# The decay gate's rank-16 stage: two-part weights side by side in one product, and the second factor in two float32r passes over 64 rows

## The chip, the cores and the metric

The kernel runs on one core of one Trainium2 chip. The metric is the time of one execution on the device in microseconds, the median over runs of the same kernel. TensorE's clock has two levels, 1.2 and 2.4 GHz; the profile gives the granted clock as a share of the upper one.

## The reference

A two-layer encoder trunk over 1024 positions and a model width of 1024, in float32. Layer 0 has two head groups (RWKV-7 time mixing and sparse attention). Layer 1 is gated linear attention (GLA) in chunks of 64 with 4 heads. Each layer ends in a residual sum and a layer norm. The change lies in the decay gate of layer 1:

```
p = h @ o_w_in
q_c, k_c, v_c, gd, g_c = split_cols(p, [512, 512, 1024, 16, 1024])
log_a = log_sigmoid(gd @ g2 + g_bias) / 16        # gd: 1024 x 16, g2: 16 x 512
b     = cumsum of log_a over the positions of a chunk
q_e, k_e = q * 128**-0.5 * exp(b), k * exp(-b)
```

So the gate is a product of rank 16: 1024 inputs to 16 numbers per position (the first factor), and these to 512 (the second factor), which then pass through a log-sigmoid, a running sum within each chunk, and two exponentials that scale the queries and keys.

## The kernel before, in words

Most large products are made in a two-part form: an operand is split into a high part rounded to float32r and the float32r remainder (`hh` and `hl` for the normed input of layer 1, `whi` and `wlo` for weights), and three products high*high, high*low and low*high are summed in PSUM. The helper `mm_fm` (lines 178 to 185) does this for a result with features on partitions: for each of 8 blocks of 128 inputs three matmuls, with the weights stationary and 512 positions streamed. `mm_tm` (lines 201 to 207) does it for a result with positions on partitions.

Layer 1 begins with the norm of layer 0 (row tile by row tile), then the first 512 columns of the values (`values(t, 0, ...)`), and then the part that the change touches, from line 1368 on:

- The 16 weight columns of the first factor are loaded to `w16` and split by a ScalarE cast (`h16`) and a VectorE subtraction (`l16`).
- `mm_fm` multiplies them with `hh` and `hl` for two halves of 512 positions: 2 x 8 x 3 = 48 matmuls with 16 columns of weights, into 16 partitions of a PSUM tile `dn`.
- ScalarE copies the 16 x 1024 result to `gdT` in plain float32 (line 1377), and `g2`, the second factor, is loaded to 16 partitions.
- For each of 4 heads two float32 matmuls over 16 rows (line 1387) give 128 x 1024 into another `dn` tile, of which there are three. ScalarE takes the absolute value (line 1390) and VectorE the minimum with zero (line 1391).
- The log-sigmoid follows on ScalarE as Exp (line 1393) and Ln (line 1395), on VectorE a subtraction, a scan, a copy and a second subtraction (lines 1397 to 1402), and on ScalarE two closing Exps (lines 1403 and 1404).
- The second 512 columns of the values, `values(t, 1, wv, "tr")`: 8 row tiles t0 to t7, each 24 matmuls into one of two PSUM banks `tr`, and a ScalarE copy out of the bank into `vg` (line 1331).
- The query and key products (lines 1414 to 1418), which VectorE multiplies by the exponentials on the way out of PSUM.

Weights come through `wload` (line 162): a DMA on SP's queue to `wraw` (three buffers), a ScalarE cast to `whi`, a GpSimd subtraction to `wlo` (twelve buffers each). The small loads `w16` and `g2` go through ScalarE's queue.

The program is written in this order, but a scheduler sets the order of instructions on each engine when the program is built: it takes them by readiness as its own model of time has it. Each engine then executes its list in order, so that a copy that stands behind other ScalarE work waits for it. The matmuls of the second factor come out between those of the values, and the copies of the values between the steps of the gate.

Of the kernel before, what the change touches and what calls it, by code (L numbers as in the profile page):

```python
# [8 lines left out]
F32 = mybir.dt.float32  # L9
F32R = mybir.dt.float32r  # L10
# [11 lines left out]
P = 128  # L22
SEQ = 1024
NT = 8
D = 1024
NK = 8
CH = 64
# [46 lines left out]
def trunk(ctx: ExitStack, tc: tile.TileContext, x, positions, e_w_in, a_mu, a_w0, a_w2, a_a0, a_a2,  # L74
          a_kk_scale, a_ka, a_rk, a_gn_g, a_gn_b, b_kv_norm_g, b_wuk, b_wuv, e_w_out, o_w_in, c_g2,
          c_g_bias, c_norm_g, o_w_out, ln_g, ln_b, out, dbg=None, stop=None):
    nc = tc.nc
    V, A, G, PE = nc.vector, nc.scalar, nc.gpsimd, nc.tensor
    f32 = lambda ap: ap.bitcast(F32)
# [56 lines left out]
    def dtile():  # L136
        return psum["pool"].tile([P, 1024], F32, name="dn", tag="dn", bufs=psum["dn"])

    def ptile(tag, bufs=None):
        return psum["pool"].tile([P, 512], F32, name=tag, tag=tag, bufs=psum["bank"].get(tag, 1))  # L140
# [37 lines left out]
    def mm_fm(pst, wb, cs, ah, al, half):  # L178

        sl = slice(half * 512, half * 512 + 512)  # L180
        for k in range(NK):
            wh, wl = wb[k]
            PE.matmul(pst, wh[:, cs], ah[:, k, sl], start=(k == 0), stop=False)  # L183
            PE.matmul(pst, wh[:, cs], al[:, k, sl], start=False, stop=False)  # L184
            PE.matmul(pst, wl[:, cs], ah[:, k, sl], start=False, stop=(k == NK - 1))  # L185
# [173 lines left out]
    for t in range(NT):  # L359
        pt = dtile()  # L360
# [12 lines left out]
    for t0 in (0, 4):  # L373
        pt = ptile("tr")
# [246 lines left out]
    def shifted(f, c0, j):  # L621
        o = st("sh", bufs=3)
        shift_out(o, proj(c0 + j * P), f + j)
        return o
# [4 lines left out]
    for j in range(3):  # L629
        for z in PG[2 * j]:  # L630
            gate(z)
        k, r, v = (shifted(f, c0, j) for f, c0 in ((4, C_K), (0, C_R), (8, C_V)))
# [89 lines left out]
    for i in range(2, NT):  # L722
# [3 lines left out]
        z = slice(i - 2, i - 1)  # L726
# [17 lines left out]
    k = shifted(4, C_K, j)  # L744
# [529 lines left out]
    for u in range(NT):  # L1274
        w = u + 2
# [39 lines left out]
    hh = hp.tile([P, NK, SEQ], F32R, name="hh")  # L1315
    hl = hp.tile([P, NK, SEQ], F32R, name="hl")
# [48 lines left out]
    lp = l_ctx.enter_context(tc.tile_pool(name="lp", bufs=1, side="right"))  # L1365


    w16 = lp.tile([P, NK, 16], F32, name="w16")
    nc.scalar.dma_start(w16, owi[:, O_GD:O_GD + 16].rearrange("(k p) c -> p k c", p=P))
    h16, l16 = lp.tile([P, NK, 16], F32R, name="h16"), lp.tile([P, NK, 16], F32R, name="l16")  # L1370
    A.copy(h16, w16)
    V.tensor_sub(l16, w16, f32(h16))
    pt = dtile()
    for half in range(2):
        mm_fm(pt[0:16, half * 512:half * 512 + 512], [(h16[:, k], l16[:, k]) for k in range(NK)], slice(0, 16), hh, hl, half)
    gdT = lp.tile([16, SEQ], F32, name="gdT")
    A.copy(gdT, pt[0:16, :])
    g2 = lp.tile([16, 512], F32, name="g2")
    nc.scalar.dma_start(g2, c_g2[0])
    m1 = lp.tile([P, SEQ], F32, name="m1")  # L1380
    V.memset(m1, 1.0)
    V.memset(m1.rearrange("p (c t) -> p c t", t=CH)[:, :, 0:1], 0.0)
# [1 line left out]
    for h in range(4):  # L1384
        pt = dtile()
        for half in range(2):
            PE.matmul(pt[:, half * 512:half * 512 + 512], g2[:, h * P:(h + 1) * P], gdT[:, half * 512:half * 512 + 512],
                      start=True, stop=True)
        bc = par[:, GBI + h:GBI + h + 1]
        A.activation(eb[:, h], pt, AF.Abs, bias=bc)  # L1390
        V.tensor_scalar(la[:, h], pt, bc, 0.0, op0=ALU.add, op1=ALU.min)
# [20 lines left out]
    for z, (c0, dst, ex) in enumerate(((O_Q, qg, la), (O_K, kg, eb))):  # L1412
        wb = wblock(w0p, owi, c0, 512, bufs=RB)
        for j in range(4):
            pt = dtile()
# [86 lines left out]
    for z in range(RB):  # L1502
        c, k = divmod(z, NK)
# [6 lines left out]
    for z in range(RB, 16):  # L1510
        c, k = divmod(z, NK)
# [57 lines left out]
```

## Time and profile before

| | |
|---|---|
| median of 3 runs | 1324.16 us (1319.51 to 1325.7) |
| profiled execution | 1315.61 us, its span 1313.9 us |
| TensorE busy | 1193.3 us, 91% of the span |
| VectorE busy | 789.9 us, 60% |
| ScalarE busy | 602.5 us, 46% |
| GpSimd busy | 442.2 us, 34% |
| mean granted clock of TensorE | 0.956 |

Instructions are named by engine (PE is TensorE's matmuls, PEld its weight loads, DVE is VectorE, ACT is ScalarE, POOL is GpSimd, SP the queue of DMAs), by the line of the kernel and by the tiles that they write and read, with digits left out of names: `h<-w` is `h16<-w16`, `tr<-whi,hh` a matmul of the values. A float32 product shows as two instructions. Matmuls are pipelined, so that their durations overlap: the time of one is read from the distance between two starts. In brackets stands the idle time of the engine before an instruction, and what ended it.

### The profile page before, as it was taken

The page shows a single profiled execution, that of the slowest core. Times are in us where ns is not written, and L with a number is a line of the kernel's source. Part 1 is how long each engine was busy: PE and PEld are TensorE (multiplying, and loading weights), DVE is VectorE, ACT ScalarE, POOL GpSimd, SP SyncE. Part 2 cuts the span into 40 slices and gives each one's busy share as a digit, 9 for nine tenths or more (in the row PEclk, how much of TensorE's full clock was granted, in tenths as well). Part 3 has the DMA queues.
Part 4 walks back from the last instruction along what each step waited for, and adds up shares of the span by engine and source line. Part 5 has one row for each costly group of instructions (what it writes and reads, how often), then busy time and mean ns, then how long its engine had stood idle before and what let it go on. Part 6 is the DMA issues. An engine that isn't in the chain of part 4 may idle for free.

```text
span 1313.9 us, 22069 instructions
## 1 busy us (share of the span) xinstructions
PE 1193.3 (91%) x8141; PEld 942.7 (72%) x8141; DVE 789.9 (60%) x1868; ACT 602.5 (46%) x1253; POOL 442.2 (34%) x749
## 2 busy tenths in 40 slices
PE   7998798899899977998988499999899999998997
PEld 6986586566666665777777388876588878887785
DVE  5246879999999546676776436680701025444666
ACT  5347777668742445666766421232920024333100
POOL 3324741453447433344455610333031231142000
PEclk9998899899899979998999599999999999999999
DMA  6102311432515487343542756652020120024221
GB/s 210 39 1 85 109 44 29 137 104 72 153 41 144 117 221 189 98 104 93 128 120 51 217 167 221 212 177 68 0 64 16 49 65 1 0 65 136 81 92 53
DMA packets 164780, 130.52 MB, mean 99 GB/s; under 512 B 61440, under 2 KB 138288, under 8 KB 164672
## 3 DMA queue, kind: packets, MB, share of 16 engines
q1 hardware_dynamic: 161872, 122.72, 32.5%
q10 hardware_dynamic: 2800, 6.39, 1.5%
q8 instruction: 64, 1.05, 0.3%
q14 instruction: 44, 0.36, 0.1%
HBM read 86.08 MB, written 42.99 MB: 98 GB/s over the span
## 4 chain that ended last, share of the span: by engine, by line
PE 47%; DVE 20%; issue 9%; DMA 8%; ACT 7%; POOL 6%; SPq 1%; DVEq 0%; POOLq 0%; ACTq 0%
DVE junk L686 7%; PE op L774 7%; PE s L774 7%; PE dn L183 3%; PE dn L185 3%; PE dn L184 3%; PE gt L207 2%; PE gt L205 2%; PE gt L206 2%; POOL wlo L92 2%; PE s L853 2%; DMA wraw<-in_e_w_in_dram 1%; PE po L876 1%; PE dn L1465 1%; DVE sc L420 1%
## 5 line engine op out<-in xcount | busy, mean ns | idle before, releaser
L92 POOL TENSOR_TENSOR wlo<-wraw,whi 128x256 fp32r<-128x256 f32 (+1 forms) x160 | 117.0, 762 | 259.8 <-ACT whi L168 217.0
L183 PE MATMUL dn<-xh,chi 128*128 128x512 f32 x336 | 137.0, 408 | 4.8 <-DVE sh L512 3.1
L185 PE MATMUL dn<-xh,clo 128*128 128x512 f32 x336 | 137.1, 408 | 0.0
L184 PE MATMUL dn<-xl,chi 128*128 128x512 f32 x336 | 135.8, 404 | 0.0
L168 ACT CAST whi<-wraw 128x512 fp32r<-128x512 f32 (+1 forms) x80 | 48.6, 612 | 139.3 <-PE dn L184 64.4
L183 PEld LDWEIGHTS dn<-xh,chi 128*128 128x128 f32 x336 | 65.6, 195 | 25.1 <-issue 6.4
L185 PEld LDWEIGHTS dn<-xh,clo 128*128 128x128 f32 x336 | 65.6, 195 | 20.3 <-issue 6.7
L92 POOL TENSOR_TENSOR clo<-craw,chi 128x256 fp32r<-128x256 f32 x84 | 77.5, 951 | 1.0
L184 PEld LDWEIGHTS dn<-xl,chi 128*128 128x128 f32 x336 | 65.3, 194 | 16.8 <-issue 3.5
L420 DVE SCALAR_TENSOR_TENSOR sc<-rl,wi_s,sc 128x384 f32<-128x384 f32 (+5 forms) x42 | 45.1, 1074 | 24.3 <-ACT rl L415 21.9
L826 DVE CUSTOM_DVE_ANT_0 p<-s,bias_s 128x512 f32<-128x512 f32 (+1 forms) x80 | 45.3, 593 | 20.9 <-PE s L825 20.5
L92 POOL TENSOR_TENSOR vg<-vg,sg 128x256 f32<-128x256 f32 x32 | 24.1, 775 | 99.7 <-DVE vg L1491 65.2
L834 ACT ACTIVATE p<-p,am 128x128 f32<-128x128 f32 (+7 forms) x64 | 49.6, 776 | 15.6 <-DVE am L832 11.1
L193 POOL CAST chi<-craw 128x1024 fp32r<-128x1024 f32 x21 | 22.7, 1080 | 97.0 <-PE dn L184 79.7
L686 DVE TENSOR_SCALAR_CACHE_REDUCE junk<-khi,Hc 128x384 bf16<-128x384 int16 (+1 forms) x64 | 51.9, 810 | 1.7
L686 DVE TENSOR_SCALAR_CACHE_REDUCE junk<-klo,Lc 128x384 bf16<-128x384 int16 (+1 forms) x64 | 51.8, 810 | 1.7
L853 PE MATMUL s<-ident,p 128*128 128x128 f32 x288 | 48.4, 293 | 4.1 <-ACT pT L855 3.2
L205 PE MATMUL gt<-whi,hh 128*128 128x512 f32 x128 | 51.9, 406 | 0.0
L774 PE MATMUL s<-whi,yh 128*128 128x512 f32 x128 | 51.2, 400 | 0.0
L774 PE MATMUL op<-whi,yh 128*128 128x512 f32 x128 | 51.2, 401 | 0.0
L207 PE MATMUL gt<-whi,hl 128*128 128x512 f32 x128 | 51.2, 400 | 0.0
L206 PE MATMUL gt<-wlo,hh 128*128 128x512 f32 x128 | 51.0, 399 | 0.0
(479 smaller groups left out, 3413.8 us busy)
## 6 DMA issues: line engine op xcount, KB each, us to landing
wraw<-in_o_w_in_dram SPq DMA_DIRECT2D x48, 256.0 KB
craw<-in_e_w_in_dram SPq DMA_DIRECT2D x21, 512.0 KB
xt<-in_x_dram SPq DMA_DIRECT2D x8, 512.0 KB
d_q<-qiT SPq DMA_DIRECT2D x8, 512.0 KB
d_ar<-ar SPq DMA_DIRECT2D x8, 512.0 KB
d_gate<-sg SPq DMA_DIRECT2D x8, 512.0 KB
qT<-d_q SPq DMA_DIRECT2D x8, 512.0 KB
AT<-d_ar SPq DMA_DIRECT2D x32, 128.0 KB
```

The costliest lines, as they stand in the source:

```text
L92: return [f(out[:, a:min(n, a + w)], *(z[:, a:min(n, a + w)] for z in ins)) for a in range(0, n, w)]
L183: PE.matmul(pst, wh[:, cs], ah[:, k, sl], start=(k == 0), stop=False)
L184: PE.matmul(pst, wh[:, cs], al[:, k, sl], start=False, stop=False)
L185: PE.matmul(pst, wl[:, cs], ah[:, k, sl], start=False, stop=(k == NK - 1))
L205: PE.matmul(pst, ah[:, k, sl], wh, start=(k == 0), stop=False)
L206: PE.matmul(pst, ah[:, k, sl], wl, start=False, stop=False)
L207: PE.matmul(pst, al[:, k, sl], wh, start=False, stop=(k == NK - 1))
L420: E.scalar_tensor_tensor(acc[:, a:b], r, w, acc[:, a:b], op0=ALU.mult, op1=ALU.add)
L686: V.tensor_scalar(junk[:, :n], x, c[:, z:z + 1], None, op0=ALU.is_ge, op1=ALU.add, accum_out=cnt[:, z:z + 1])
L774: ins = PE.matmul(pt, a[:, k, :], b, start=(k == 0 and z == 0), stop=(k == NK - 1 and z == 2))
L834: A.activation(ps[k][:, :n], ps[k][:, :n], AF.Exp, scale=0.125, bias=m[:, k:k + 1], accum_out=rsum[:, k:k + 1])
L853: inorder(PE.transpose(pt[:, j * P:(j + 1) * P], OUT[i]["ps"][2 * j + s][:, kt * P:(kt + 1) * P], ident))
```

## The change

The weights of the first factor stand in one tile `w64` of 64 columns: high part, low part, and both again. One product with `hh` and `hl` (32 matmuls) gives 64 rows: high times x, low times x, and these again, so that all four products of the parts are made. The 64 rows are then cut into a float32r operand `gdx`: rows 0 to 31 are the rounded values, rows 32 to 63 the remainder of the same values. The second factor is loaded four times, to 64 partitions, and split into `g2h` and `g2l`; each head sums two float32r passes over these 64 rows. The diff:

```
-    h16, l16 = lp.tile([P, NK, 16], F32R, name="h16"), lp.tile([P, NK, 16], F32R, name="l16")
-    A.copy(h16, w16)
-    V.tensor_sub(l16, w16, f32(h16))
+
+    w64 = lp.tile([P, NK, 4, 16], F32R, name="w64")
+    for z in (0, 2):
+        A.copy(w64[:, :, z], w16)
+        V.tensor_sub(w64[:, :, z + 1], w16, f32(w64[:, :, z]))
+
+    g2 = lp.tile([CH, 512], F32, name="g2")
+    nc.scalar.dma_start(g2, bass.AP(tensor=c_g2[0].tensor, offset=c_g2[0].offset, ap=[[0, 4], [512, 16], [1, 512]]))
+    g2h, g2l = lp.tile([CH, 512], F32R, name="g2h"), lp.tile([CH, 512], F32R, name="g2l")
+    A.copy(g2h, g2)
+    V.tensor_sub(g2l, g2, f32(g2h))
     pt = dtile()
     for half in range(2):
-        mm_fm(pt[0:16, half * 512:half * 512 + 512], [(h16[:, k], l16[:, k]) for k in range(NK)], slice(0, 16), hh, hl, half)
-    gdT = lp.tile([16, SEQ], F32, name="gdT")
-    A.copy(gdT, pt[0:16, :])
-    g2 = lp.tile([16, 512], F32, name="g2")
-    nc.scalar.dma_start(g2, c_g2[0])
+        sl = slice(half * 512, half * 512 + 512)
+        for k in range(NK):
+            for z, x_ in enumerate((hh, hl)):
+                PE.matmul(pt[0:CH, sl], w64[:, k].rearrange("p z c -> p (z c)"), x_[:, k, sl], start=(k == 0 and z == 0),
+                          stop=(k == NK - 1 and z == 1))
+
+    gdx = lp.tile([CH, SEQ], F32R, name="gdx")
+    gdh = lp.tile([CH, SEQ], F32R, name="gdh")
+    A.copy(gdh, pt[0:CH])
+    A.copy(gdx[0:32], pt[0:32])
+    V.tensor_sub(gdx[32:CH], pt[32:CH], f32(gdh[32:CH]))
...
         for half in range(2):
-            PE.matmul(pt[:, half * 512:half * 512 + 512], g2[:, h * P:(h + 1) * P], gdT[:, half * 512:half * 512 + 512],
-                      start=True, stop=True)
+            for z, w in enumerate((g2h, g2l)):
+                PE.matmul(pt[:, half * 512:half * 512 + 512], w[:, h * P:(h + 1) * P], gdx[:, half * 512:half * 512 + 512],
+                          start=(z == 0), stop=(z == 1))
```

## Rows read from the trace of the kernel before

**Rows 1.** The page's busy time, share of the span and instructions, TensorE first.

```profile
PE 1193.3 (91%) x8141; PEld 942.7 (72%) x8141; DVE 789.9 (60%) x1868; ACT 602.5 (46%) x1253; POOL 442.2 (34%) x749
```

**Rows 2.** Busy time by stretches; columns are named in the first line.

```profile
core 0: us, PE busy (x) PEld busy (x) DVE busy (x) ACT busy (x) POOL busy (x), PEclk, DMA share, GB/s
...
919.90:925.30 5.40, 5.40 (x14) 2.16 (x13) 1.39 (x2) 3.87 (x5) 0.00 (x0) 1.00 0.00 0
925.30:929.00 3.70, 3.70 (x10) 2.92 (x10) 2.58 (x3) 3.66 (x4) 0.00 (x0) 0.54 0.00 0
...
950.90:973.40 22.50, 22.46 (x96) 18.14 (x97) 1.36 (x4) 7.08 (x11) 5.14 (x7) 1.00 0.05 13
973.40:1062.00 88.60, 88.60 (x381) 71.04 (x379) 8.57 (x7) 10.42 (x17) 22.86 (x33) 1.00 0.18 48
1062.00:1196.00 134.00, 132.62 (x631) 111.43 (x630) 55.01 (x153) 44.45 (x126) 33.79 (x47) 1.00 0.10 30
```

**Rows 3.** TensorE's matmuls in order of time: start us, us, engine, line, tiles, shapes.

```profile
903.22 0.41 PE L183 MATMUL dn<-hh,h 128*16 128x512 f32 x1 [1.37 <-ACT vg L1331]
...
914.26 0.39 PE L205 MATMUL tr<-whi,hh 128*128 128x512 f32 x1
...
919.95 5.41 PE L1387 MATMUL dn<-gdT,g 16*128 16x512 f32 x12
...
926.05 0.63 PE L207 MATMUL tr<-whi,hl 128*128 128x512 f32 x1
...
930.98 1.98 PE L1387 MATMUL dn<-gdT,g 16*128 16x512 f32 x4
...
942.87 0.50 PE L205 MATMUL tr<-whi,hh 128*128 128x512 f32 x1 [1.78 <-ACT vg L1331]
...
950.94 0.50 PE L205 MATMUL tr<-whi,hh 128*128 128x512 f32 x1 [1.96 <-ACT vg L1331]
...
973.44 0.39 PE L184 MATMUL dn<-hl,whi 128*128 128x512 f32 x1
```

**Rows 4.** Matmuls by tile; ns min/median/max, first and last start.

```profile
L183 PE MATMUL dn<-hh,h x16: 388/388/410, 903.2 to 913.6; 128*16 128x512 f32 x16
...
L1387 PE MATMUL dn<-gdT,g x16: 587/587/692, 919.9 to 932.4; 16*128 16x512 f32 x16
```

**Rows 5.** ScalarE in order of time, columns as in rows 3.

```profile
896.28 0.59 ACT L1331 COPY vg<-ca 128x512 f32<-128x512 f32 x1 [5.01 <-PE ca L207]
...
914.51 1.00 ACT L1377 COPY gdT<-dn 16x1024 f32<-16x1024 f32 x1 [5.16 <-PE dn L185]
...
921.96 1.11 ACT L1390 ACTIVATE kg<-dn,par 128x1024 f32<-128x1024 f32 x1 [1.32 <-PE dn L1387]
...
925.18 1.28 ACT L1395 ACT_TABLE_LOAD   x1
926.48 1.06 ACT L1395 ACTIVATE kg<-kg 128x1024 f32<-128x1024 f32 x1
...
942.25 0.57 ACT L1331 COPY vg<-tr 128x512 f32<-128x512 f32 x1
...
950.32 0.56 ACT L1331 COPY vg<-tr 128x512 f32<-128x512 f32 x1
...
953.79 0.57 ACT L1331 COPY vg<-tr 128x512 f32<-128x512 f32 x1
```

**Rows 6.** ScalarE's groups by form: busy us, mean ns of one, idle before.

```profile
L1395 ACT ACT_TABLE_LOAD x4 | 5.1, 1283 | 0.1
...
L1393 ACT ACTIVATE kg<-kg 128x1024 f32<-128x1024 f32 x4 | 4.2, 1062 | 0.1
L1395 ACT ACTIVATE kg<-kg 128x1024 f32<-128x1024 f32 x4 | 4.2, 1059 | 0.0
...
L1393 ACT ACT_TABLE_LOAD x2 | 2.6, 1283 | 0.0
L1403 ACT ACT_TABLE_LOAD x2 | 2.6, 1283 | 0.0
```

**Rows 7.** VectorE in order of time, columns as in rows 3.

```profile
923.17 1.28 DVE L1391 TENSOR_SCALAR qg<-dn,par 128x1024 f32<-128x1024 f32 x1 [34.00 <-ACT kg L1390]
```

## The prediction

> **What bounds the kernel now.** First the busy shares: TensorE is busy for 1193.3 of 1313.9 us [rows 1], so the end moves with TensorE unless a wait elsewhere sets it. Then the table by stretches [rows 2]. The stage that the change touches lies between 903.22, where TensorE starts the first product, and 973.44, where the query product takes over. Behind it TensorE is busy for all 88.6 us from 973.4 to 1062 and for 132.6 of the next 134.0, and the weight loads there are released by TensorE's own matmuls, so I take what this stage gains or loses to reach the end in full. I call this stage S; its length is 70.22 us.
>
> The order of TensorE's work in S [rows 3]: 48 matmuls of the first product (903.22 to 914.26), the second half of the values (8 row tiles t0 to t7, 24 matmuls each), and inside these the second product, heads 0 to 2 at 919.95 and head 3 at 930.98. Twice TensorE stands idle inside S, before 942.87 (1.78 us) and before 950.94 (1.96 us), both times for ScalarE's copy of a values tile out of PSUM. There are two such banks, so t3 waits for the copy of t1 and t4 for that of t2.
>
> ScalarE is the second thing to read [rows 5, 6]. From 921.96 on it works without a break through the gate's chain: per head Abs, Exp, Ln and two closing Exps, 20 operations of some 1.05 us, and eight table loads of 1.28, because Exp and Ln come in turns. The copy of t1 stands behind 12 of these 20 and starts at 942.25, when TensorE has run through t2 and waits for it; that of t2 behind 17, at 950.32. So in S either TensorE's sum or ScalarE's chain can be what ends last, and the change shortens only the first directly.
>
> **The change part by part, against the profiled execution.** Its time is 1315.61 us with a span of 1313.9; the median of the three runs, 1324.16, is 8.55 higher, and my predicted time is that median less the gain.
>
> First product. Removed are 48 matmuls at (914.26 - 903.22) / 48 = 0.230 us each, 11.04 in all [rows 3, 4]. Added are 32, each with 64 columns of weights. Their streamed side, 512 columns, is unchanged, and matmuls with 16 columns (0.230) and with 128 columns (22.5 us for 96, so 0.234, [rows 2]) bound the new one from both sides. I take 0.230: 7.36 us, a gain of 3.68. At 0.234 it would be 0.13 less.
>
> Second product. Removed are 8 float32 products. Each shows as two instructions, 16 in all [rows 4], 12 of which run from 919.95 over 5.34 us and 4 from 930.98 over 1.91 (to the next values matmul); with the two steps of 0.1 us ahead of them 7.44 us. Added are 16 float32r matmuls with 64 rows of weights. No float32r matmul with 64 rows is in the trace. The 128-row ones at 0.234 are the nearest; the float32 instruction at 0.43 is the other bound (16 x 0.43 = 6.9). I take 0.233: 3.73 us, a gain of 3.71, with 0.5 as its lower bound.
>
> Clock. Behind heads 0 to 2 the granted clock falls to a mean of 0.54 from 925.3 to 929.0 [rows 2], which is the lower level of 1.2 GHz nearly throughout: nine values matmuls stand 0.427 us apart instead of 0.233 the second of them is in [rows 3]. What TensorE did before was float32 work on 16 of 128 rows for 5.4 us. The first product, which also fills only 16 of 128 columns, kept 2.4 GHz for 11 us. The change replaces the float32 stretch by 2.8 us of work on 64 rows. I take the fall to be gone: 9 x 0.194 = 1.75 us gained; nothing gained is the other bound, and a fall that stays is rival D.
>
> Operand preparation. Two casts and two subtractions in place of one each, a wider transfer of the second factor's weights, one cast and one subtraction of these. They fall between 886 and 897, where ScalarE sits idle for five us at a stretch ([rows 5], at 896.28) and VectorE for 34 [rows 7]; the product that needs them starts at 903.22. I cost them at nothing. Without that cover it would be some 1.5 us for ScalarE's three casts, at no more than the 0.58 us of a 512-column copy each.
>
> Between the products. One ScalarE copy of 1.00 us ([rows 5], at 914.51) becomes two copies of that size and a subtraction, which I put at 1.28 by the 1024-column VectorE operation out of PSUM [rows 7]. The rounding error part needs the first copy, so the operand is ready some 2.8 us behind the first product's end instead of 1.3. Queued behind the copies on ScalarE is nothing but the gate's chain. TensorE has t0 to do meanwhile, 24 x 0.233 = 5.6 us, as it had before, so this also costs nothing; if the second product were put directly behind the first, it would cost 2.8.
>
> Sum for TensorE alone: S becomes 7.36 + 3.73 + 192 x 0.2333 (44.8) = 55.9 us, and the values end at 959.1. Before, they ended at 973.44 less the four query matmuls (0.93) that had been pulled ahead, so 972.5. If no wait were left, the gain would be 13.4.
>
> What is late next: t1's copy. With the order of before, TensorE ends the first product at 910.6, t0 at 916.2, head 0 at 917.1, heads 0 to 2 at 919.0, t1 and head 3 at 925.5, t2 at 931.1. ScalarE's chain starts some 0.3 behind head 0 as now, at 917.4 instead of 921.96. What counts is how many chain operations stand ahead of t1's copy. Before, a head arrived every 1.72 us while Abs took 1.1, so each gap was filled by the next step of an older head, and this mixed Exp with Ln. With a head every 0.93 us the three Abs can follow one another, and then four Exps and four Lns group, with one table load instead of six ahead of t1's copy. In that order, 4 x 1.1 + 4 x 1.06 + 1.30 + 4 x 1.06 = 14.2 us and the copy's 0.5 [rows 5, 6] put its end at 932.1. TensorE then waits 1.0 us at t3, and t4 to t7 find their banks free. The values end at 932.1 + 5 x 5.6 = 960.1: a gain of 12.4. If the first head's closing Exps come ahead of the copy as they did before, that adds a load and two operations, 3.4 us, and the gain is 9.0. I take a value between them nearer to the first, 11.0: 1304.6 for a profiled execution, and 1313.2 against the median.
>
> The Trainium skill (ScalarE: Activation LUTs, section "What ACT_TABLE_LOAD costs") gives a switch of tables 1283 ns and a drain of some 1380 behind it. The trace has the 1.28 [rows 5], and the Ln behind it starts 1.30 us after the load does, so no drain shows here; by the page the one load ahead of the copy would cost 1.4 more and the upper gain would be 11.0 instead of 12.4.
>
> The Trainium skill (TensorE: Matmul & The Clock Gate, Part 3, "The mechanism") has weight loads overlap a running matmul only where their row groups differ. All loads here use the same rows as the matmul that runs, and yet matmuls stand 0.234 us apart with a load between each pair [rows 2], so the trace does not follow it; by the page the new 64-row matmuls would each wait for their load, by an estimate some 0.19 each from the load's share of that row (18.14 us for 97), 3.0 us in all, and the gain would be 8.0.
>
> **The rivals.**
>
> B, ScalarE's order stays as it is. Then the chain alone shifts, by 4.56 us: t1's copy ends at 938.3 (20.9 behind the start, as before), t2's at 946.3, t3's at 949.8. TensorE waits 7.2 us at t3 and 2.4 at t4, and the values end at 968.8: a gain of 3.7, 1320.4. For it: the order is made for the whole program and was close to alternating. Against it: that alternation came from the slow arrival of heads, which goes.
>
> C, slower: the copy of t1 falls behind the whole gate chain, which stands ahead of it in the program. Before, 12 of 20 operations were ahead of it, and 17 ahead of t2's. With all heads ready early nothing need leave a gap for it. 20 operations (21.3), eight loads (10.4) and the copy end at 917.4 + 32.2 = 949.6, t3 starts there, and the values end at 977.6: 5.1 longer, 1329.3. It decides once t1's copy ends later than 944.5, 27 us behind the chain's start. Against it: both early copies were placed soon after an operation of the chain had to wait for VectorE, and those waits stay.
>
> D, the clock still falls to 1.2 GHz around the second product: 16 x 0.194 = 3.1 there and 1.75 behind it are lost, the gain is 6.1, 1318.0. For it: this is the one place inside S where it falls. Against it: four times the rows and half the time.
>
> That the change doesn't do what it says (64-row float32r passes at the float32 price) is 3.2 off the gain, 1316.4, and lies inside the range.
>
> **How the numbers follow.** Forecast 0.56, with its own range of 9.0 to 13.4 gained, 1310.8 to 1315.2; B 0.20, C 0.12, D 0.12. 0.5% of the time is 6.6 us, about what a measurement of this kernel tells from no change. Faster by more: the forecast and a third of D, 0.60. Within it: B and the rest of D, 0.28. Slower: C, 0.12. The range runs from the full 13.4 with 3.8 for the spread of a median (the three runs lie 6.2 apart), 1307, to B with 2.6 of it, 1323, and leaves C out.
>
> **What would show it.** Right: 32 first-product matmuls in some 7.4 us; the second product's 16 at 0.233; no granted clock under 1.00 in S; two to four table loads in the chain instead of eight; at most one wait of TensorE for a values copy, under 4 us; the query product starting around 960 to 963. Wrong: a wait of 7 us at t3 with eight loads (B), a query product after 973 (C), values matmuls 0.43 apart (D), or a change outside S as large as the one inside.

## The result, and the profile after

The changed kernel takes 1308.98 us (median of 4 runs, 1301.1 to 1311.88) against 1323.2 us (4 runs, 1319.51 to 1325.7): a ratio of 0.9885, 95% interval 0.9836 to 0.9935. A second set on another occasion, 6 runs against 11, gave 1304.47 against 1317.18, a ratio of 0.9896 with 0.9875 to 0.9918. So the change saves some 14 us, 1.1%, with an interval from 0.8 to 1.25% by the narrower set.

The profiled execution of the changed kernel took 1311.88 us, only 3.7 less than that of before. The span and the engines' busy time, after:

```profile
span 1310.2 us, 22044 instructions
...
PE 1189.9 (91%) x8125; PEld 945.8 (72%) x8125; DVE 792.5 (60%) x1871; ACT 602.2 (46%) x1254; POOL 442.9 (34%) x749
```

The stage itself says more. TensorE in order of time, after; these rows answer to [rows 3] (start us, us, engine, line, tiles; in brackets the idle time ahead):

```profile
910.69 0.44 PE L1386 MATMUL dn<-hh,w 128*64 128x512 f32 x1 [1.41 <-ACT vg L1331]
...
918.13 0.40 PE L205 MATMUL tr<-whi,hh 128*128 128x512 f32 x1
...
925.83 0.40 PE L205 MATMUL tr<-whi,hh 128*128 128x512 f32 x1
926.16 0.50 PE L1402 MATMUL dn<-gdx,g2h 64*128 64x512 f32 x1
926.49 0.39 PE L1402 MATMUL dn<-gdx,g2l 64*128 64x512 f32 x1
...
928.79 0.39 PE L1402 MATMUL dn<-gdx,g2l 64*128 64x512 f32 x1
929.10 0.50 PE L206 MATMUL tr<-wlo,hh 128*128 128x512 f32 x1
929.44 0.40 PE L207 MATMUL tr<-whi,hl 128*128 128x512 f32 x1
...
958.76 0.50 PE L205 MATMUL tr<-whi,hh 128*128 128x512 f32 x1 [0.32 <-ACT vg L1331]
...
970.05 0.40 PE L183 MATMUL dn<-hh,whi 128*128 128x512 f32 x1
```

The first product starts at 910.69 instead of 903.22, and the query product takes over at 970.05 instead of 973.44. The stage S lasts 59.36 us instead of 70.22. Nine query matmuls were pulled into it instead of four, which is work done, so I count V: S less 0.233 us for each of these. V is 57.26 us after and 69.29 before, a difference of 12.0. What lies behind hardly changed: from the start of the query product to the end of the span 340.1 us after, 340.5 before. So the five more query matmuls that were pulled ahead (1.2 us) made the rest only 0.35 us shorter, and from the start of the first product to the end of the span the gain is 11.2 us (410.7 to 399.5) where V says 12.0.

ScalarE in the stage, after, as in [rows 5]:

```profile
918.38 1.01 ACT L1391 CAST gdh<-dn 64x1024 fp32r<-64x1024 f32 x1 [1.80 <-PE dn L1386]
919.29 1.00 ACT L1392 CAST gdx<-dn 32x1024 fp32r<-32x1024 f32 x1
...
927.38 2.12 ACT L1405 ACTIVATE kg<-dn,par 128x1024 f32<-128x1024 f32 x2 [2.87 <-PE dn L1402]
...
932.42 1.28 ACT L1410 ACT_TABLE_LOAD   x1
933.72 1.06 ACT L1410 ACTIVATE kg<-kg 128x1024 f32<-128x1024 f32 x1
934.79 1.28 ACT L1408 ACT_TABLE_LOAD   x1
...
937.05 0.57 ACT L1331 COPY vg<-tr 128x512 f32<-128x512 f32 x1
```

The first two steps of the gate (Abs, Exp) now follow at the pace of ScalarE. The copy of t1 is at 937.05, 9.7 us behind the chain's start, with two table loads ahead of it; before, it was at 20.3 us with six [rows 5]. The granted clock by stretches, after, beside [rows 2]:

```profile
core 0: us, PE busy (x) PEld busy (x) DVE busy (x) ACT busy (x) POOL busy (x), PEclk, DMA share, GB/s
910.60:918.10 7.50, 7.41 (x32) 4.42 (x33) 0.00 (x0) 2.52 (x5) 6.79 (x10) 1.00 0.54 147
...
926.10:929.10 3.00, 3.00 (x13) 2.14 (x13) 0.50 (x1) 1.72 (x2) 0.00 (x0) 1.00 0.00 0
929.10:935.70 6.60, 6.60 (x28) 4.91 (x27) 4.16 (x4) 6.55 (x7) 0.00 (x0) 1.00 0.00 0
935.70:970.10 34.40, 34.08 (x146) 27.13 (x146) 18.14 (x22) 24.84 (x29) 5.17 (x8) 1.00 0.03 9
```

It is 1.00 throughout, where before it fell to 0.54 behind the heads.

The 12.0 us add up from the starts of matmuls: the first product 11.04 to 7.44 (3.6), the second with the slower steps into and out of it 7.64 to 4.47 (3.2), the clock (eight matmuls at 0.427 instead of 0.233) 1.5, the waits for copies of values with the slower steps around them 4.3 to 0.6 (3.7).

### The profile page after: what moved, and what is told of

It reads as the page before. It is cut to its first block, busy times and chain, and to the rows that moved or that the text cites. A ratio compares the mean times of both kernels' runs of the same rounds, so it can differ in the third digit from the quotient of the medians.

```text
span 1310.2 us, 22044 instructions
## 1 busy us (share of the span) xinstructions
PE 1189.9 (91%) x8125; PEld 945.8 (72%) x8125; DVE 792.5 (60%) x1871; ACT 602.2 (46%) x1254; POOL 442.9 (34%) x749
## 4 chain that ended last, share of the span: by engine, by line
PE 43%; DVE 23%; DMA 10%; issue 10%; ACT 6%; POOL 5%; SPq 2%; DVEq 0%; POOLq 0%; ACTq 0%
DVE junk L686 7%; PE op L774 7%; PE s L774 3%; PE dn L185 2%; PE dn L183 2%; PE dn L184 2%; PE gt L207 2%; PE gt L206 2%; PE gt L205 2%; PE s L853 2%; DMA wraw<-in_e_w_in_dram 2%; POOL wlo L92 1%; PE po L876 1%; DMA z<-d_h 1%; PE dn L1480 1%
## 5 line engine op out<-in xcount | busy, mean ns | idle before, releaser
L774 PE MATMUL s<-wlo,yh 128*128 128x512 f32 x128 | 51.3, 401 | 0.0
```

The lines of the kernel that those rows point to most:

```text
L774: ins = PE.matmul(pt, a[:, k, :], b, start=(k == 0 and z == 0), stop=(k == NK - 1 and z == 2))
```

## The experiments

All are read by V, since the time ahead of the stage scatters. The first four below were timed once each, in the order of the table 1310.32, 1315.55, 1312.07 and 1319.86 us against 1323.14 for the kernel before; single times say little here, as runs of one kernel lie six to ten apart. V over all profiles, with the start of the first product, TensorE's idle time at values copies, and where the clock was at its lower level:

| kernel | first product starts | V, us | waits, us | lower clock |
|---|---|---|---|---|
| before | 903.22 | 69.29 | 1.78 + 1.96 | 925.6 to 929.0 |
| before, 2nd | 904.46 | 70.88 | 0.17 + 1.98 | 925.7 to 932.6, 953.0 to 956.5 |
| before, 3rd | 905.37 | 69.28 | 1.77 + 1.97 | 927.5 to 930.9 |
| changed | 910.69 | 57.26 | 0.32 | none |
| changed, 2nd | 904.88 | 57.26 | 0.30 | none |
| first product alone | 903.36 | 64.29 | 2.60 | 940.7 to 944.1 |
| second product alone | 910.56 | 60.96 | 0.32 | none |
| float32r over 16 rows | 906.28 | 61.92 | none | 926.3 to 929.8 |
| before, Exp for Ln | 908.52 | 68.40 | none | 927.7 to 938.0 |
| one pass of 128 rows | 903.22 | 54.16 | none | none |

**The first product alone** (lines taken out and put in against the changed kernel).

```
+    g2s = lp.tile([CH, 512], F32, name="g2s")
+    A.activation(g2s, g2, AF.Copy, scale=0.5)
...
-    V.tensor_sub(gdx[32:CH], pt[32:CH], f32(gdh[32:CH]))
+    gdx = lp.tile([CH, SEQ], F32, name="gdx")
+    A.copy(gdx, pt[0:CH])
...
+            PE.matmul(pt[:, half * 512:half * 512 + 512], g2s[:, h * P:(h + 1) * P], gdx[:, half * 512:half * 512 + 512],
+                      start=True, stop=True)
```

> First product as changed (32 matmuls, 64 columns), second factor in float32 as before but over all 64 rows (its weights halved, as each part stands there twice). Measure: V, the time from the first product's first matmul to the end of the values, less the query matmuls pulled ahead: 69.3 us before, 57.3 after. Theory (four separate terms: first product 3.6, second product 3.2, clock 1.7, waits for values copies 3.8; the waits go because heads arrive quickly): the heads arrive at the old pace, so eight table loads and both waits stay, V = 65.7 if the clock falls again, 64.0 if it doesn't. Rival (the shorter first product alone takes TensorE out of step with ScalarE and the waits go): V about 60 to 62. On the clock: if 16 rows made it fall, the granted clock stays 1.00 here; if float32 did, it falls to 0.5 for some 3.5 us behind heads 0 to 2.

V was 64.29 us. TensorE's rows, then the start of ScalarE's chain and its copy of t1:

```profile
916.48 5.41 PE L1397 MATMUL dn<-gdx,g2s 64*128 64x512 f32 x12
921.83 0.50 PE L205 MATMUL tr<-whi,hh 128*128 128x512 f32 x1
922.16 0.40 PE L206 MATMUL tr<-wlo,hh 128*128 128x512 f32 x1
922.40 0.40 PE L207 MATMUL tr<-whi,hl 128*128 128x512 f32 x1
...
939.41 0.50 PE L205 MATMUL tr<-whi,hh 128*128 128x512 f32 x1 [2.60 <-ACT vg L1331]
...
941.06 0.63 PE L205 MATMUL tr<-whi,hh 128*128 128x512 f32 x1
941.49 0.63 PE L206 MATMUL tr<-wlo,hh 128*128 128x512 f32 x1
```

```profile
918.50 1.11 ACT L1400 ACTIVATE kg<-dn,par 128x1024 f32<-128x1024 f32 x1 [1.33 <-PE dn L1397]
...
938.79 0.57 ACT L1331 COPY vg<-tr 128x512 f32<-128x512 f32 x1
```

The same 5.4 us of float32 as before, over 64 rows, and the values behind it stand 0.24 us apart from the second on: no fall of the clock there. As the heads arrive at the old pace, ScalarE again has eight table loads, and t1's copy starts 20.3 us behind the chain's start, as in [rows 5]. One wait of 2.6 us stays, and behind that wait the clock does fall (0.427 us between the last two rows of TensorE). 3.6 for the product, 1.5 for the clock behind the heads and 1.4 of waits, less some 1.5 for the clock behind the wait, make the 5.0 that are gone. V came near the 64.0 of the theory by two misses that cancel: one wait less, and a fall of the clock behind the other. The rival, that a shorter first product ends the waits by itself, is refuted for t1's copy and holds for t2's: the second wait did go, as t2's copy stands behind 14 operations of the chain here and not behind 17.

**The second product alone** (against the changed kernel).

```
+    for z in range(4):
+        A.activation(wh4[:, :, z], w16, AF.Copy, scale=0.5)
+        V.scalar_tensor_tensor(wl4[:, :, z], w16, 0.5, f32(wh4[:, :, z]), op0=ALU.mult, op1=ALU.subtract)
...
-                PE.matmul(pt[0:CH, sl], w64[:, k].rearrange("p z c -> p (z c)"), x_[:, k, sl], start=(k == 0 and z == 0),
-                          stop=(k == NK - 1 and z == 1))
+        mm_fm(pt[0:CH, half * 512:half * 512 + 512], [(wh4[:, k].rearrange("p z c -> p (z c)"), wl4[:, k].rearrange("p z c -> p (z c)"))
+                                                      for k in range(NK)], slice(0, CH), hh, hl, half)
```

> First product in 48 matmuls in three parts as before, but with its columns four times over (weights halved) so that 64 rows result; second factor in two float32r passes over 64 rows as changed. Theory of four terms: V = 69.3 - 3.2 - 1.7 - 3.8 = 60.6 us, no granted clock under 1.00, six table loads, waits of TensorE for a values copy under 1 us in all. Rival (the waits go only with the shorter first product): V about 64.4, with some 4 us of waits.

V was 60.96 us, the clock 1.00, the one wait 0.32. TensorE's row:

```profile
962.32 0.50 PE L205 MATMUL tr<-whi,hh 128*128 128x512 f32 x1 [0.32 <-ACT vg L1331]
```

8.3 of the 12.0 us come with the second product: its own 3.2, the clock and the waits. It is 3.7 above the changed kernel, which is the first product. The order of ScalarE from the first Abs on is that of the changed kernel, step by step, so it comes with the second product, whose heads arrive faster, and not with the first. The pace of the heads is the likely reason; the order is not set by it alone, for with heads as fast over 16 rows (below) t1's copy stands behind 10 operations and three loads, not behind 7 and two.

**Float32r passes over 16 rows** (this and the versions below against the kernel before).

```
-    gdT = lp.tile([16, SEQ], F32, name="gdT")
+    gdT = lp.tile([16, SEQ], F32R, name="gdT")
...
+    A.copy(g2h, g2)
+    V.tensor_sub(g2l, g2, f32(g2h))
...
+            for z, w in enumerate((g2h, g2l)):
+                PE.matmul(pt[:, half * 512:half * 512 + 512], w[:, h * P:(h + 1) * P], gdT[:, half * 512:half * 512 + 512],
+                          start=(z == 0), stop=(z == 1))
```

> First product as before (48 matmuls, 16 columns). Second factor in two float32r passes over 16 rows; the remainder of the first product's result is left out. If float32 is what made the clock fall: V = 60.6 us as with 64 rows, clock 1.00 throughout. If the 16 rows did: nine or so values matmuls behind the heads at 0.427 us, V = 62.3, or less where only 2.8 us of such work is too short a stretch.

V was 61.92. TensorE's rows around the end of heads 0 to 2, and the two stretches:

```profile
925.49 0.38 PE L1391 MATMUL dn<-gdT,g2h 16*128 16x512 f32 x1
925.71 0.38 PE L1391 MATMUL dn<-gdT,g2l 16*128 16x512 f32 x1
926.03 0.56 PE L205 MATMUL tr<-whi,hh 128*128 128x512 f32 x1
926.39 0.63 PE L206 MATMUL tr<-wlo,hh 128*128 128x512 f32 x1
926.81 0.63 PE L207 MATMUL tr<-whi,hl 128*128 128x512 f32 x1
...
```

```profile
923.00:926.00 3.00, 3.00 (x13) 2.12 (x12) 0.48 (x1) 2.27 (x3) 0.00 (x0) 1.00 0.00 0
926.40:929.40 3.00, 3.00 (x9) 2.32 (x8) 2.57 (x3) 2.98 (x5) 0.00 (x0) 0.50 0.00 0
```

The clock falls to 1.2 GHz behind 2.9 us of float32r work on 16 rows as it did behind 5.4 us of float32 on 16 rows, and it did not fall behind either kind on 64 rows. So here the fall goes with the 16 rows and not with the type. It came behind the heads or within them in all five profiles with 16 rows, and in none of the four with 64. One thing is not told apart: in those five the first product has 16 columns too, and in those four 64, and no run has 16 columns with 64 rows. Against the columns speaks that the clock is 1.00 through the whole first product and through 5.7 us of values behind it.

**The kernel before with Exp in place of Ln.**

```
-        A.activation(eb[:, h], eb[:, h], AF.Ln, bias=1.0)
+        A.activation(eb[:, h], eb[:, h], AF.Exp, bias=1.0)
```

> The kernel before with Exp in place of Ln in the gate, so that no table is loaded between them; values of the gate change, its instructions and their order on every engine do not. Theory (the copies of values were late by the six table loads of 1.28 ahead of t1's copy and eight ahead of t2's): both waits of TensorE go, V = 69.3 - 4.2 = 65.1 us, and the clock still falls behind heads 0 to 2. Rival (their place behind 12 and 17 chain operations is enough to make them late): at least one wait of over 1.5 us stays, V over 67.

Both waits went, as the theory has it, and V was still 68.40. TensorE's rows and the stretches of its clock:

```profile
925.32 8.25 PE L1387 MATMUL dn<-gdT,g 16*128 16x512 f32 x12
933.50 0.80 PE L205 MATMUL tr<-whi,hh 128*128 128x512 f32 x1
934.09 0.63 PE L206 MATMUL tr<-wlo,hh 128*128 128x512 f32 x1
...
```

```profile
925.30:927.50 2.20, 2.20 (x6) 1.03 (x6) 0.00 (x0) 0.75 (x2) 0.00 (x0) 1.00 0.00 0
928.00:938.00 10.00, 10.00 (x18) 5.20 (x17) 7.91 (x7) 8.57 (x9) 0.00 (x0) 0.50 0.00 0
```

In this execution the clock fell already in the middle of the heads and stayed low for 10 us: heads 0 to 2 took 8.18 us instead of 5.34, and the eleven steps behind them 4.70 instead of 2.57, where before nine took 3.75 instead of 2.10. That is 2.84 + 0.48 = 3.3 us which the profile of before does not have. Without them V would be 65.1, as expected. A slower TensorE also leaves the copies more time, but by less than the margins that they had: t1's copy ended 5.4 us before t3 started (944.24 and 949.63), t2's 5.4 before t4 (950.05 and 955.46). So the waits show that the table loads made the copies late; that V is then 65.1 is worked out.

**The two kernels again**, to tell what scatters.

> The kernel before, another execution. If the change's gain is in its own stage and the rest is scatter ahead of it: the first product starts anywhere between 903 and 911 us, the stage V (first product's first matmul to the end of the values, less query matmuls pulled ahead) takes 69.3 us plus what the clock costs more or less, and the values' end lies 340 to 341 us ahead of the end. The clock falls behind heads 0 to 2 again; where it falls for some 10 us instead of 3.5, as it did without Ln, V is about 72.5. Rival (the 7.5 us that the changed kernel's first product started later belong to the change): the start is at 903 to 904 again.

> The kernel before, a third execution: as for the second. V between 69.3 and 72.5 us, depending on how long the clock stays at its lower level.

> The changed kernel again, timed in five rounds. Theory (12.0 us of V in the profiled pair, and 0 to 3 more where the clock stays low for longer in the kernel before): 12 to 15 us faster, a ratio of 0.9885 to 0.991. V = 57.3 us as in its first profile, no granted clock under 1.00 in it. Rival (the change also costs something ahead of its stage): the difference is 4 to 8 us, and the first product starts at 910 or later again.

The changed kernel's second profile has V = 57.26 again, and its first product starts at 904.88; the kernel before starts it at 904.46 and 905.37. TensorE's rows of the changed kernel's second profile:

```profile
904.88 0.45 PE L1386 MATMUL dn<-hh,w 128*64 128x512 f32 x1 [1.35 <-ACT vg L1331]
...
952.94 0.50 PE L205 MATMUL tr<-whi,hh 128*128 128x512 f32 x1 [0.30 <-ACT vg L1331]
...
964.24 0.40 PE L183 MATMUL dn<-hh,whi 128*128 128x512 f32 x1
```

So the 7.5 us by which its first profile came late into the stage are scatter: up to the change's own preparation every engine's list of instructions ahead of the stage is the same in both kernels, and the start lies between 903 and 911 us over all ten profiles. The two profiles stood 4.1 us apart at 30 us, where the input is loaded, and 4.0 at 784, with swings between; the rest came between 784 and 894 us, where the layer norms run. The kernel before has V = 69.28 and 70.88; in the second profile the clock fell 1.6 us before the end of heads 0 to 2, stayed low for 6.8 us, and fell once more behind the wait of 1.98:

```profile
921.25 6.20 PE L1387 MATMUL dn<-gdT,g 16*128 16x512 f32 x12
...
944.17 0.50 PE L205 MATMUL tr<-whi,hh 128*128 128x512 f32 x1 [0.17 <-ACT vg L1331]
...
952.24 0.49 PE L205 MATMUL tr<-whi,hh 128*128 128x512 f32 x1 [1.98 <-ACT vg L1331]
...
953.87 0.63 PE L207 MATMUL tr<-whi,hl 128*128 128x512 f32 x1
954.29 0.63 PE L205 MATMUL tr<-whi,hh 128*128 128x512 f32 x1
```

The gain in V by these pairs is 12.0 to 13.6 us, and from the start of the first product to the end of the span 10.8 to 12.3. The timed difference, 13.7 us (10.8 to 16.5 by its interval), agrees with both.

**One pass of 128 rows**, a version beyond the change.

```
+    w64 = lp.tile([P, NK, 8, 16], F32R, name="w64")
+    for z in (0, 2, 4, 6):
...
+    A.copy(g2w[0:CH], g2[0:CH])
+    V.tensor_sub(g2w[CH:P], g2[CH:P], f32(g2h[CH:P]))
...
+    for z in (0, CH):
+        A.copy(gdx[z:z + 32], pt[z:z + 32])
+        V.tensor_sub(gdx[z + 32:z + CH], pt[z + 32:z + CH], f32(gdh[z + 32:z + CH]))
...
-            PE.matmul(pt[:, half * 512:half * 512 + 512], g2[:, h * P:(h + 1) * P], gdT[:, half * 512:half * 512 + 512],
+            PE.matmul(pt[:, half * 512:half * 512 + 512], g2w[:, h * P:(h + 1) * P], gdx[:, half * 512:half * 512 + 512],
                       start=True, stop=True)
```

> A step further: the first factor's weights eight times over (128 columns), the second factor's high part on rows 0 to 63 and its low part on rows 64 to 127, so that one float32r pass of 128 rows per half does what two of 64 did: 8 matmuls less. Theory (V is TensorE's sum): V = 57.3 - 8 x 0.233 + 32 x 0.003 = 55.5 us, 1.8 us less than the change, too little for the timed runs to tell apart (0.14%). Rival (two more ScalarE copies of 1.0 us and one more subtraction ahead of the heads delay them, the order of ScalarE shifts and a wait for a values copy returns): V of 57 or more.

V was 54.16, 3.1 below the change, where 1.8 were expected. The time was 1301.59 us (6 runs), a ratio to the kernel before of 0.9884, 0.9858 to 0.9910; that overlaps the change's 0.9875 to 0.9918, so the timed runs do not tell the two apart. TensorE's rows:

```profile
921.05 0.40 PE L207 MATMUL tr<-whi,hl 128*128 128x512 f32 x1
921.28 1.53 PE L1403 MATMUL dn<-gdx,g2w 128*128 128x512 f32 x6
922.65 0.39 PE L205 MATMUL tr<-whi,hh 128*128 128x512 f32 x1
```

Six matmuls in 1.37 us, and no gap on either side. In the changed kernel the first step into the 64-row heads takes 0.33 us (925.83 to 926.16), the second 0.33 (to 926.49), and the two steps out of them 0.31 and 0.34 instead of 0.233; over both groups of heads that is 0.74 us more than the matmuls alone. Here it is gone, as is the wait of 0.3 with the slower steps around it (0.6); less 0.1 for the wider first product and with the 1.87 of eight matmuls, that makes the 3.1.

## Why the prediction was right

It was right in sign and size: 1313.2 forecast, 1308.98 measured, inside 1307 to 1323. The forecast gain was 11.0; V gained 12.0 in the profiled pair and up to 13.6 against other executions of the kernel before, of which 11.2 and up to 12.3 reached the end of the span. The 11.0 was picked between 12.4 and 9.0, so that it came this close is in part luck. By its steps:

- The path: what the stage gains reaches the end. From the start of the query product to the end of the span it is 339.9 to 340.5 us in all five profiles of the two kernels. What does not reach it is the work pulled ahead into S.
- First product: 3.68 forecast, 3.6 measured. Its 64 columns cost what 16 and 128 bounded.
- Second product: 3.71 forecast, 3.2 measured. The 64-row matmuls stand 0.23 us apart, but entering and leaving them costs 0.74 us in all, which I had left out; of the old product's 0.39 I had counted half.
- Clock: 1.75 forecast, 1.5 measured in that pair, and the fall goes with the 16 rows, with the 16 columns of the first product as the rival that no run tests. What I did not see is that the clock stays low for 3.4 or 6.8 us in the three profiles of the kernel before, and for 10.2 in the one with Exp for Ln, so that this term is worth 1.5 to 3.1 us, and 4.9 there.
- Operand preparation: nothing forecast, and TensorE's idle time ahead of the first product is 1.41 us after and 1.37 before.
- Waits: the forecast had ScalarE's chain starting 14.2 us behind the first product's start, with four Exps and four Lns in groups, and t1's copy behind 12 operations and one load, to end 28.9 us behind that start. In fact 34 values matmuls precede the heads, not 24, the chain starts at 16.7, six table loads remain (two to four were named as a sign of being right), and t1's copy stands behind 7 operations and two loads and ends at 26.9. The one wait that is left is not that of t3 for t1's copy, as forecast, but that of t6 for t4's (TensorE's row at 958.76), and five query matmuls fill 1.2 us ahead of it. So the step as put was wrong, and that its sum (one wait of 1.0 or less) came out as 0.3 is luck. What held is that the copies come early enough once the heads no longer take 0.86 us per half, as the second product alone shows.
- The two rules of the Trainium skill. The Trainium skill (ScalarE: Activation LUTs, section "What ACT_TABLE_LOAD costs") adds a drain of some 1380 ns to the load. None shows here on either side of a load: the load at 932.42 takes 1.28 and its Ln starts at 933.72, and the load at 934.79 starts where that Ln of 1.06 ends. The Trainium skill (TensorE: Matmul & The Clock Gate, Part 3, "The mechanism") has loads overlap a running matmul only where their row groups differ, though it also names a background weight buffer, which the rows cannot show. Here 64-row matmuls with a load each stand 0.23 us apart, and each load inside the group starts 0.23 ahead of its matmul, so it overlaps work on the same rows; the 3.0 us more that the forecast worked out by that rule did not come.

Rival B (ScalarE's order stays) and D (the clock still falls) are refuted by the profile after; their mechanisms are real, as the first product alone and the 16-row passes show. C (copies behind the whole chain) did not come: t1's copy ended 10.2 us behind the chain's start, far from the 27 from which it decides. One sign of being wrong did show in the first profile, a change outside S nearly as large as the one inside (the 7.5 us); the second profile shows that it is scatter. The profiled execution of before, 1315.61, lay below the timed runs shown with it, and that of after, 1311.88, was the longest of its four: whoever compared these two alone would have read 3.7 us.

## What to carry to other kernels

Read a change of ten microseconds from the stage's own start and end in the profile, where runs of one kernel lie six to ten apart; count out the work pulled into it, and look at the rest behind, whether that work shortened it. A small product over few rows can cost more than its own time: through the clock behind it, and, in float32, through the slow pace at which it feeds a chain on another engine, which here went with more table loads and so with the waits that came back to TensorE. Look whether two passes over half the rows fit into one over all of them: that took another 3.1 us off the stage here, too little for the timed runs to tell.

## What the runs showed of the hardware that was not expected

- In five of five profiles whose second product works on 16 of 128 rows the granted clock went to 1.2 GHz, behind heads 0 to 2 or within them, with float32 (5.4 us) and float32r (2.9 us) alike, and stayed there for 3.4 to 10.2 us. With the same work on 64 rows it stayed at 2.4 GHz, four of four. Whether the 16 columns of the first product, which go with the 16 rows, have a part in it is open.
- Behind an idle time of 2.60 us and one of 1.98 the clock fell also; behind others of 1.77 to 1.97 it did not (four times in two profiles).
- Between float32r matmuls of 128 rows and of 64 or 16 the step is 0.31 to 0.34 us instead of 0.233, twice on the way in and twice on the way out; between 128-row matmuls of different products it stays at 0.23. The weight loads go with it: within a group a load starts 0.23 us ahead of its matmul, and where the number of rows changes it starts together with it. The first two loads of the 64-row heads, after, whose matmuls start at 926.16 and 926.49:

```profile
926.15 0.18 PEld L1402 LDWEIGHTS dn<-gdx,g2h 64*128 64x128 f32 x1 [0.37 <-issue]
926.26 0.19 PEld L1402 LDWEIGHTS dn<-gdx,g2l 64*128 64x128 f32 x1
```
